# First norm by blocks in turn with small weight pieces, six buffers of weight parts, priorities for some operations, and a merge moved off GpSimd

## The chip, the cores and the metric

The kernel runs on one core of one Trainium2 chip. A core has a matrix engine (TensorE, PE in the profile, with its weight loads as PEld), a vector engine (VectorE, DVE), a scalar engine (ScalarE, ACT), GpSimd (POOL), SyncE (SP, which only issues DMAs here) and 16 DMA engines. Engines run their own instruction queues in order and wait for each other by semaphores. The metric is the device time of one execution in microseconds (us).

## The reference

Two layers (DEPTH 2) of 256 tokens by 1024 channels, float32. Each layer is

```
x = x + 0.5 * swiglu(rmsnorm(x), w_gu (1024 x 5632), w_down (2816 x 1024))
h = rmsnorm(x);  one projection h @ w_in (1024 x 5962)
y_a = 6 heads of attention with forget gates (softmax)
y_b = 5 heads of stick-breaking attention (no softmax; logs and cumulative sums)
y_c = 5 heads of sparse attention (an indexer picks 64 keys a row; softmax)
merged = sig(g_a) * (y_a @ w_up_fox) + sig(g_b) * (y_b @ w_up_sb) + sig(g_c) * (y_c @ w_up_dsa)
x = x + merged @ w_out
x = x + 0.5 * swiglu(rmsnorm(x), ...)        # second pair of weights
```

and a last rmsnorm follows the second layer. All weights, some 205 MB, are read once from HBM as float32.

## The kernel before

**Products.** Every float32 operand of a large product is split into two float16 parts, hi and lo, and the product is three matmuls: hi by hi, hi by lo, lo by hi. `split` (L247) makes the parts: hi on ScalarE (L249), lo on VectorE (L251), for weights (`whi`, `wlo`, read from `raw`) and activations alike. In most products the weight is the stationary operand (a 128 x 128 block) and the activation, 256 tokens wide and transposed (channels on partitions), moves; `project_T` (L317) does these, with three matmuls of 256 columns for each block of weights (L339). `project` (L363) has the tokens stationary.

**Weights.** The list `chunks` (L174) names the weight blocks in the order of use, mostly 1024 rows by 512 columns. Each is cut in raw loads of 4 row blocks (k = 0 to 3, 4 to 7, 1 MB each; the first chunk is cut finer, L206) and each raw load in pieces, at most 2048 columns a partition. `advance(i)` (L274) runs when piece i is about to be used: it emits the splits of the pieces up to i + HL_BUFS, and raw DMAs up to RAW_BUFS ahead of the last split. HL_BUFS is 4 (pairs of parts), RAW_BUFS 5 (L200).

**Order.** The program is laid out by Python; a scheduler then orders each engine's queue, taking among the operations that its own model holds ready the one that was emitted first. `behind` (L143) adds an order edge with no wait. `high_priority`, not used in the kernel before, puts what is emitted in it ahead of earlier emitted work that is ready too. `Task` (L283) wraps a generator of small work; `background()` (L307) steps the first two tasks after every two row blocks of a product (`every`, L349), and `finish` runs one to its end at that place.

**Feed-forward.** `ffn` (L613) computes for each of six column chunks the gate product g, scales it by the row of reciprocal norms R and takes the silu (L632, L633), then the up product u and their product (L638), which is split to `ah`, `al`; then the down product, whose result is added to the transposed residual `xT` (`add_T`, L645 to L649). PSUM tiles: four of tag mm for the products, two tp and two at for the rest.

**Norms.** `Norm.half(h)` (L519) makes `xThi`, `xTlo` of one half of the channels as soon as `xT` is there, without the row scale; `stats` (L529) sums squares, by `acc` (L537, L539) and a matmul (`ss`, L546), takes the power on GpSimd (L469) and `rows_of` (L496) spreads it to R by a matmul (`rb`, L503). `norm.finish()` (L628, L765) forces all of that right after the first product that uses the norm. `FirstNorm` (L581) does the first norm from the untransposed x: `split_half` (L471) transposes four blocks of 128 tokens on PE, applies the gain on VectorE (L483), splits 512 columns, and copies to `xT` (L486); two such for each half of the channels. Five matmuls on an identity (`warm`, L424) precede them.

**Mixer.** `mixer` (L748) runs the groups of w_in, with the attention as tasks: `indexer`, `latent`, `forget` (L916, it ends in the `cps` matmuls, L931), and the heads in pairs. A pair makes its operands `T`, `M`, `W` (`operands`, L795 to L810), yields twice, runs the scores (L833), the softmax (L970, whose last step, L980, scales by the reciprocal sum on VectorE), transposes (L986) and multiplies by the values (L959). Then the gates, the three up products, merged by L1140 and L1142 (the second of three merges on GpSimd), the split to `mT`, and w_out with its residual (L1151).

Of the kernel before, what the change touches and what calls it, by code (L numbers as in the profile page):

```python
# [10 lines left out]
F32 = mybir.dt.float32  # L11
# [118 lines left out]
def trunk(ctx, tc, io, out, flag):  # L130
# [69 lines left out]
    RAW_BUFS, HL_BUFS = (4, 6) if wide else (5, 4)  # L200
    raws, pieces, chunk_pieces = [], [], []
    for ci, (nm, l, r, c, n) in enumerate(chunks):
# [3 lines left out]
        cuts = [0, 1, 2, 4, 6, 8] if ci == 0 else list(range(0, nk, rk)) + [nk]  # L206
# [15 lines left out]
    start, raw_dma = {}, []  # L222
# [33 lines left out]
    def emit_piece():  # L256
# [10 lines left out]
        a, b = split(hv, lv, src, sw, guard and guard.weight())  # L267
        if i in start:
            for j, k in zip((a, b), start[i]):
                behind(j, *k)  # L270
        hl_tiles[i] = (hv, lv)
        state["piece"] += 1

    def advance(i):  # L274

        while state["piece"] < min(len(pieces), i + HL_BUFS):
            emit_piece()
        last = pieces[state["piece"] - 1][0]
        while state["raw"] < min(len(raws), last + RAW_BUFS):
            emit_raw()  # L280
# [141 lines left out]
    warm = att("warm")  # L422
    for i in range(5):
        nc.tensor.matmul(warm[:, :P], ident, ident, start=True, stop=True)  # L424
# [46 lines left out]
    def split_half(src, t, h, hi, lo, gcol, nm, keep):  # L471

        ps = tpt("xp" + nm)
        for j in range(4):
            k = 4 * h + j
            i = nc.tensor.transpose(ps[:, j * P:(j + 1) * P], src[:, t, k * P:(k + 1) * P], ident)
            if h == 1:
                behind(i, state["last"])
        pv = ps.rearrange("p (j c) -> p j c", j=4)
        tmp = t512("xg" + nm)  # L480
        pv2 = tmp.rearrange("p (j c) -> p j c", j=4)
        g = gT[:, gcol + 4 * h:gcol + 4 * h + 4]
        i = nc.vector.tensor_tensor(pv2, pv, g[:, :, None].to_broadcast([P, 4, P]), op=ALU.mult)  # L483
        start.setdefault(0, ((), (i,)))
        r = split(hi[:, 4 * h:4 * h + 4, t * P:(t + 1) * P], lo[:, 4 * h:4 * h + 4, t * P:(t + 1) * P], pv2, 1.0, None)
        behind(nc.scalar.copy(keep, pv), r[0])  # L486
        return r

# [7 lines left out]
    def rows_of(rstd, nm):  # L496

        dg = sp.tile([P, NT, P], F32, tag="kcT", name="dg" + nm)
        for t in range(NT):
            nc.vector.tensor_scalar(dg[:, t, :], ident, rstd[:, t:t + 1], None, op0=ALU.mult)  # L500
        yield
        ps = tpt("rb" + nm)
# [722 lines left out]
```

## Time and profile before

| | |
|---|---|
| median of 3 runs | 1169.36 us (1167.49 to 1169.77) |
| profiled execution | 1170.57 us, of which the span of the trace is 1168.8 |
| busy PE, PEld, DVE, ACT, POOL | 1125.8, 962.6, 792.4, 603.6, 30.0 us |
| mean granted TensorE clock | 0.987 |
| DMA | 209.96 MB, mean 180 GB/s |

Matmuls are pipelined and their ends are modelled: a PE that is busy all of a stretch can still be at half of its rate. How many matmuls a stretch holds, and the clock granted in it, say more. An engine's idle time has a price only where another engine waits for it.

### The profile page before, as it was taken

Reading aid. Unit: us, or ns where it says so; the run is one execution under the profiler, and the core shown is the slowest. Engines: PE = TensorE matmul, PEld = TensorE weight load, DVE = VectorE, ACT = ScalarE, POOL = GpSimd, SP = SyncE. Lnnn points to the kernel's source line nnn. Section 1 sums busy time; section 2 is a strip of 40 time slices with the busy share of each in tenths; the row PEclk is TensorE's granted clock in tenths of the full one; section 3 lists DMA queues with packets and bytes.
Section 4 is the critical chain, followed back from the end, with each engine's and each line's share of the span. In section 5 each row is a group of like instructions: output and inputs, shape, how many; then the busy total and the mean of one; then the engine's idle time right before and its main releaser. Section 6 shows DMA issues by size and latency. Waiting matters only on the chain.

```text
span 1168.8 us, 22864 instructions
## 1 busy us (share of the span) xinstructions
PE 1125.8 (96%) x9736; PEld 962.6 (82%) x9736; DVE 792.4 (68%) x1387; ACT 603.6 (52%) x790; POOL 30.0 (3%) x33
## 2 busy tenths in 40 slices
PE   7999999989999899999999999999999989999996
PEld 5888887777888788888888888867788878888765
DVE  5665655898786866565566565579977698566653
ACT  6544543656566554453454454456556665544531
POOL 0000000000001100000000000000000020000000
PEclk8999999989999999999999999999999999999999
DMA  9755655455434766565656566555453267565731
GB/s 343 239 164 191 227 166 184 147 180 176 132 109 134 230 199 188 161 225 199 217 189 199 163 217 208 163 168 164 166 178 113 91 197 236 182 180 180 245 100 40
DMA packets 118723, 209.96 MB, mean 180 GB/s; under 512 B 4770, under 2 KB 43860, under 8 KB 118612
## 3 DMA queue, kind: packets, MB, share of 16 engines
q1 hardware_dynamic: 118292, 207.88, 55.2%
q8 instruction: 78, 1.28, 0.5%
q10 hardware_dynamic: 320, 0.53, 0.1%
q14 instruction: 33, 0.27, 0.1%
HBM read 207.35 MB, written 1.05 MB: 178 GB/s over the span
## 4 chain that ended last, share of the span: by engine, by line
PE 78%; DVE 13%; ACT 4%; issue 2%; DMA 1%; POOL 0%; POOLq 0%; DVEq 0%; ACTq 0%; SPq 0%
PE uw_ffn_gu L339 20%; PE gw_ffn_gu L339 18%; PE gt L339 9%; PE d0w_ffn_down L339 7%; PE d512w_ffn_down L339 7%; DVE wlo L251 7%; ACT whi L249 3%; PE up L339 2%; PE in L339 2%; PE o L339 1%; PE ya L959 1%; DVE isc L886 1%; DMA raw<-in_w_ffn_gu_dram 1%; PE sa L151 1%; PE in L376 1%
## 5 line engine op out<-in xcount | busy, mean ns | idle before, releaser
L251 DVE SCALAR_TENSOR_TENSOR wlo<-raw,whi 128x2048 f16<-128x2048 f32 (+6 forms) x229 | 459.6, 2009 | 273.0 <-ACT whi L249 267.5
L339 PEld LDWEIGHTS <-whi 128*128 128x128 f16 x5504 | 539.8, 98 | 77.2 <-issue 9.6
L249 ACT ACTIVATE whi<-raw 128x2048 f16<-128x2048 f32 (+6 forms) x229 | 379.1, 1660 | 422.3 <-issue 122.5
L339 PEld LDWEIGHTS <-wlo 128*128 128x128 f16 x2768 | 272.4, 98 | 41.0 <-issue 4.9
L339 PE MATMUL gw_ffn_gu<-xThif,whi 128*128 128x256 f16 x704 | 193.5, 276 | 4.3 <-ACT xThif L249 4.3
L339 PE MATMUL gw_ffn_gu<-xTlof,whi 128*128 128x256 f16 x704 | 194.0, 276 | 1.3 <-DVE xTlof L525 0.7
L339 PE MATMUL uw_ffn_gu<-xThif,whi 128*128 128x256 f16 x704 | 192.0, 273 | 1.9 <-ACT whi L249 1.9
L339 PE MATMUL gw_ffn_gu<-xThif,wlo 128*128 128x256 f16 x704 | 193.7, 276 | 0.0
L339 PE MATMUL uw_ffn_gu<-xThif,wlo 128*128 128x256 f16 x704 | 192.1, 273 | 0.0
L339 PE MATMUL uw_ffn_gu<-xTlof,whi 128*128 128x256 f16 x704 | 192.0, 273 | 0.0
L339 PE MATMUL gt<-xThimx,whi 128*128 128x256 f16 x384 | 104.8, 273 | 0.0
L339 PE MATMUL gt<-xThimx,wlo 128*128 128x256 f16 x384 | 104.7, 273 | 0.0
L339 PE MATMUL gt<-xTlomx,whi 128*128 128x256 f16 x384 | 104.7, 273 | 0.0
L339 PE MATMUL d0w_ffn_down<-ahw_ffn_gu,wlo 128*128 128x256 f16 x264 | 72.0, 273 | 0.0
L339 PE MATMUL d0w_ffn_down<-alw_ffn_gu,whi 128*128 128x256 f16 x264 | 72.0, 273 | 0.0
L339 PE MATMUL d512w_ffn_down<-ahw_ffn_gu,whi 128*128 128x256 f16 x264 | 72.0, 273 | 0.0
L339 PE MATMUL d512w_ffn_down<-ahw_ffn_gu,wlo 128*128 128x256 f16 x264 | 72.0, 273 | 0.0
L339 PE MATMUL d0w_ffn_down<-ahw_ffn_gu,whi 128*128 128x256 f16 x264 | 72.0, 273 | 0.0
L339 PE MATMUL d512w_ffn_down<-alw_ffn_gu,whi 128*128 128x256 f16 x264 | 72.0, 273 | 0.0
L339 PE MATMUL in<-xThimx,whi 128*128 128x256 f16 x176 | 49.2, 280 | 0.0
L339 PE MATMUL in<-xTlomx,whi 128*128 128x256 f16 x176 | 49.0, 278 | 0.0
L339 PE MATMUL in<-xThimx,wlo 128*128 128x256 f16 x176 | 48.9, 278 | 0.0
(328 smaller groups left out, 1376.6 us busy)
## 6 DMA issues: line engine op xcount, KB each, us to landing
raw<-in_w_ffn_gu_dram SPq DMA_DIRECT2D x62, 1024.0 KB, 5.2
raw<-in_w_ffn_down_dram SPq DMA_DIRECT2D x39, 1024.0 KB, 5.1
raw<-in_w_in_dram SPq DMA_DIRECT2D x26, 1024.0 KB, 5.0
raw<-in_w_ffn_gu_dram SPq DMA_DIRECT2D x32, 768.0 KB, 4.6
raw<-in_w_in_dram SPq DMA_DIRECT2D x12, 768.0 KB, 4.4
raw<-in_w_out_dram SPq DMA_DIRECT2D x8, 1024.0 KB, 5.1
raw<-in_w_ffn_down_dram SPq DMA_DIRECT2D x7, 512.0 KB, 3.9
raw<-in_w_in_dram SPq DMA_DIRECT2D x4, 896.0 KB, 4.8
```

Source lines behind the costliest of these rows:

```text
L151: return behind(nc.tensor.matmul(*a, **k), first)
L249: a = nc.scalar.activation(hv, src, AF.Copy, scale=scale)
L251: return a, nc.vector.scalar_tensor_tensor(lv, src, scale, plain(hv), op0=ALU.mult, op1=ALU.subtract, **more)
L339: m = nc.tensor.matmul(o, u, v[:, k, :], start=(k == 0 and q == 0 and b % 2 == 0), stop=(end and q == len(ops) - 1))
L376: state["last"] = nc.tensor.matmul(o, b, wh, start=False, stop=(k == lastk))
L886: nc.vector.match_replace(out=sc[:, a:b], in_to_replace=m8, in_values=sc[:, a:b], imm_value=TAKEN)
L959: m = nc.tensor.matmul(o, v(h, ks), w[:, i * P:(i + 1) * P], start=(i == 0), stop=(i == 2))
```

## The change

- Six buffers of weight parts, HL_BUFS 4 to 6; RAW_BUFS stays 5.
- The first chunk is cut 1, 1, 1, 1, 2, 2 row blocks, the second 2, 2, 2, 2.
- The first norm goes by blocks of 128 channels and all 256 tokens: four transposes for two blocks, hi straight from PSUM on ScalarE with the gain as scale, lo on VectorE, without the separate gain step; each block is followed in both queues by the splits of one weight piece (`begin`). Blocks 4 to 7 begin when row block 3 of the first product is due; until then no more pieces are emitted (`hold`). Copies to `xT` and squares follow after the last block.
- Nine warming matmuls in place of five, and four more after the second set of transposes.
- Of the other norms, parts are emitted with high priority, the sums of squares directly, and the matmuls `ss` and `rb` two background steps later each; a norm is forced only where it is needed (`need`), and the gate's scale and silu of the first chunk are emitted during the u product (`gate`), at the latest at its row block 4.
- High priority for `add_T`, for the merges and splits after the up products, and for the residual after w_out.
- The merge of branch 1 runs on VectorE in place of GpSimd; the softmax's last scaling on ScalarE in place of VectorE.
- Heads yield three times, not two, between operands and scores.

```diff
-    RAW_BUFS, HL_BUFS = (4, 6) if wide else (5, 4)
+    RAW_BUFS, HL_BUFS = (4, 6) if wide else (5, 6)
-        cuts = [0, 1, 2, 4, 6, 8] if ci == 0 else list(range(0, nk, rk)) + [nk]
+        cuts = [0, 1, 2, 3, 4, 6, 8] if ci == 0 else [0, 2, 4, 6, 8] if ci == 1 else list(range(0, nk, rk)) + [nk]
-        while state["piece"] < min(len(pieces), i + HL_BUFS):
+        while state["piece"] < min(state.get("hold", len(pieces)), i + HL_BUFS):
-    for i in range(5):
-        nc.tensor.matmul(warm[:, :P], ident, ident, start=True, stop=True)
+    warm_up(9)
     class Norm:
+        def parts(self, k, src):
+            g = gT[:, self.gcol + k:self.gcol + k + 1]
+            return (nc.scalar.activation(self.hi[:, k, :], src, AF.Copy, scale=g),
+                    nc.vector.scalar_tensor_tensor(self.lo[:, k, :], src, g, plain(self.hi[:, k, :]),
+                                                   op0=ALU.mult, op1=ALU.subtract))
         def half(self, h):
-            for k in range(4 * h, 4 * h + 4):
...
+            with tc.high_priority():
+                for k in range(4 * h, 4 * h + 4):
+                    self.parts(k, xT[:, k, :])
+        def need(self, rows):
+            while self.R is None and (rows or self.rstd is None):
+                self.task.step()
     class FirstNorm(Norm):
+        def block(self, k):
+            q, j = k // 2, k % 2
+            if j == 0:
+                self.ps[q] = (tpt if q < 2 else att)(f"xp{self.nm}_{q}")
+                for i in range(2):
+                    for t in range(NT):
+                        m = nc.tensor.transpose(self.ps[q][:, i * SEQ + t * P:i * SEQ + (t + 1) * P],
+                                                x[:, t, (k + i) * P:(k + i + 1) * P], ident)
+                        if q > 1:
+                            behind(m, state["last"])
+                if q == 1:
+                    warm_up(4, m)
+            r = self.parts(k, self.ps[q][:, j * SEQ:(j + 1) * SEQ])
...
+        def begin(self, ks=range(4)):
+            for k in ks:
+                for r in (self.block(k), state["piece"] < HL_BUFS and emit_piece()):
+                    for i, j in zip(r or (), self.last):
+                        behind(i, j)
+                    self.last = r or self.last
+            if k == 3:
+                state["hold"] = state["piece"]
+            else:
+                self.task = Task(self.stats())
+        def ready(self, k):
+            if k == 3 and state.pop("hold", None):
+                self.begin(range(4, 8))
...
-            norm.finish()
+            def gate(k):
+                if s or (norm.R is None and k < 4):
+                    return
...
-            project_T(gu, l, DFF + c, n, (norm.hi, norm.lo), u)
+            project_T(gu, l, DFF + c, n, (norm.hi, norm.lo), u, gate)
...
-                for i, b, w in widths(n):
-                    add_T(c // P + b, w, d[i], norm.by_row(w))
+                with tc.high_priority():
+                    for i, b, w in widths(n):
+                        add_T(c // P + b, w, d[i], norm.by_row(w))
...
-                nc.vector.tensor_scalar(p[:, a:b], p[:, a:b], rsum[:, i:i + 1], None, op0=ALU.mult)
+                act(p[:, a:b], p[:, a:b], AF.Copy, scale=rsum[:, i:i + 1])
...
-            for _ in range(2):
+            for _ in range(3):
                 yield
...
-                        (nc.gpsimd if b == 1 else nc.vector).tensor_tensor(v0, v0, v, op=ALU.add)
+                            nc.vector.tensor_tensor(v0, v0, v, op=ALU.add)
...
+            with tc.high_priority():
+                for i in range(2):
+                    xs = xT[:, 4 * h + 2 * i:4 * h + 2 * i + 2, :]
+                    nc.vector.scalar_tensor_tensor(xs, pair(ps[i], 2), 1.0 / (sw * sm), xs, op0=ALU.mult, op1=ALU.add)
```

## Rows read from the trace of the kernel before

**Rows 1.** The page's first part: busy us of each engine, share of the span, instructions.
```profile
PE 1125.8 (96%) x9736; PEld 962.6 (82%) x9736; DVE 792.4 (68%) x1387; ACT 603.6 (52%) x790; POOL 30.0 (3%) x33
```

**Rows 2.** Stretches: length, busy us (count) PE, PEld, DVE, ACT, POOL; clock, DMA share, GB/s.
```profile
30.00:135.00 105.00, 105.00 (x961) 93.82 (x960) 68.12 (x94) 52.91 (x49) 0.00 (x0) 1.00 0.64 203
...
280.00:365.00 85.00, 84.33 (x756) 74.07 (x755) 59.95 (x124) 54.04 (x103) 0.00 (x0) 1.00 0.38 121
365.00:405.00 40.00, 35.75 (x324) 31.35 (x322) 35.52 (x51) 21.30 (x22) 8.57 (x4) 1.00 0.72 237
```

**Rows 3.** Chain that ended last, in order of time: start, us, what.
```profile
40.04 10.48 PE gw_ffn_gu L339 x96
```

**Rows 4.** Timeline of the start: start, us, engine, line, operation, count [idle before <-releaser].
```profile
1.82 2.50 PE L424 MATMUL warm<-ident 128*128 128x128 f32 x10 [1.82 <-POOL ident masks.py:199]
...
8.03 0.38 PE L339 MATMUL gw_ffn_gu<-xThif,whi 128*128 128x256 f16 x2 [1.66 <-ACT xThif L249]
...
18.61 0.28 PE L339 MATMUL uw_ffn_gu<-xThif,whi 128*128 128x256 f16 x1 [1.93 <-ACT whi L249]
...
21.83 0.58 PE L339 MATMUL gw_ffn_gu<-xThif,whi 128*128 128x256 f16 x2 [2.61 <-ACT xThif L249]
```

**Rows 5.** One microsecond of the start, columns as in rows 2.
```profile
24.00:25.00 1.00, 1.00 (x7) 0.67 (x6) 0.96 (x4) 0.00 (x0) 0.00 (x0) 0.50 1.05 389
```

**Rows 6.** PE's waits, whole span: line <- releaser: us in total, times, longest.
```profile
PE sa L833 <- DVE Wa L809: 4.1, 2, 2.1
PE o L339 <- DVE wlo L251: 2.9, 2, 1.4
PE o L339 <- DVE mT L251: 2.6, 2, 1.3
PE ssf L546 <- DVE accf L539: 2.5, 3, 1.1
...
PE o L339 <- DVE gt L1140: 1.8, 2, 0.9
PE up L339 <- DVE gt L1140: 1.3, 2, 0.7
...
PE rbmx L503 <- DVE dgmx L500: 1.2, 2, 0.6
PE cps L931 <- issue: 1.1, 1, 1.1
PE cps L931 <- DVE fr L926: 1.1, 1, 1.1
```

**Rows 7.** Four microseconds after three of these waits, columns as in rows 2.
```profile
250.00:254.00 4.00, 4.00 (x17) 3.17 (x16) 3.09 (x9) 1.85 (x5) 0.00 (x0) 0.50 0.66 194
...
418.00:422.00 4.00, 4.00 (x25) 3.16 (x26) 2.21 (x4) 0.00 (x0) 0.70 (x1) 0.65 0.35 133
...
822.00:826.00 4.00, 4.00 (x22) 3.22 (x21) 3.64 (x11) 1.85 (x5) 0.00 (x0) 0.58 0.64 207
```

**Rows 8.** Timeline at the first layer's up products, columns as in rows 4.
```profile
367.13 1.22 DVE L251 SCALAR_TENSOR_TENSOR wlo<-raw,whi 128x1024 f16<-128x1024 f32 x1 [0.51 <-ACT whi L249]
...
370.41 4.02 POOL L1142 TENSOR_TENSOR gt<-gt 128x512 f32<-128x512 f32 x2 [147.42 <-DVE gt L1140]
...
373.23 2.29 DVE L251 SCALAR_TENSOR_TENSOR wlo<-raw,whi 128x1024 f16<-128x1024 f32 x1
```

**Rows 9.** Groups of instructions, shapes apart: count | busy us, mean ns | idle before.
```profile
L251 DVE SCALAR_TENSOR_TENSOR wlo<-raw,whi 128x512 f16<-128x512 f32 x10 | 6.8, 683 | 6.2 <-PE cb L151 4.9 <-ACT whi L249 1.3
...
L525 DVE SCALAR_TENSOR_TENSOR xTlof<-xT,gT,xThif 128x256 f16<-128x256 f32 x24 | 10.0, 479 | 0.0
...
L980 DVE TENSOR_SCALAR pa<-pa,rsa 128x256 f32<-128x256 f32 x12 | 4.2, 346 | 0.0
...
L759 ACT ACTIVATE pa<-sa,nxa 128x256 f32<-128x256 f32 x12 | 5.6, 467 | 3.5 <-DVE nxa L975 3.5
```

**Rows 10.** ACT's longest waits within the softmax, columns as in rows 6.
```profile
ACT pc L759 <- DVE nxc L975: 11.3, 14, 1.7
```

## What the change was predicted to do, before its result was known

> **What bounds the kernel now.** I read the busy totals first. PE is busy 96% of the span and no other engine reaches 70% [rows 1]; so what counts is where PE does not run at its rate. The rate is in the chain that ended last: 96 matmuls in 10.48 us, 0.109 us each [rows 3]. The table by stages then says where this holds. From 30 to 135 us PE is busy all the time at clock 1.00, with VectorE at 68 of 105 us [rows 2]: here nothing can be gained but by doing less work. In the attention with the gates (280 to 365) PE misses 0.7 of 85 us. Around the up products (365 to 405) PE misses 4.3 of 40 us while VectorE is busy 35.5: that stretch is VectorE's [rows 2]. The start and the joints between stages are the third kind, so I read the timeline of the start and then the list of PE's waits.
>
> A busy PE can hide lost time. The Trainium skill ("Perfetto Trace Analysis", section Identifying the Most-Contended Engine) says to judge TensorE's headroom by the busy share of its weight loads, not of its matmuls. The steady stretch has 93.82 of 105 us, 0.894, the whole 962.6 of 1168.8, 0.824 [rows 1, 2]: by that rule some 92 us are off the steady rate, where PE's idle time gives 43. Part of it is matmuls of another shape, so I take neither as what can be won; I count waits one by one.
>
> The profiled execution took 1170.57 us (span 1168.8 and 1.8 around it), 1.2 above the median of 1169.36. The sum is made against 1170.57.
>
> **A. The start.** The second gate chunk begins at 40.04 [rows 3]. Before it lie two chunks of 96, 21.0 us of matmuls, and the first of them begins at 8.03 [rows 4]; so 11.0 us are lost in between. Two holes are plain: a wait of 1.93 for a weight part that ScalarE makes 2048 columns at a time, and one of 2.61 for the second half of the norm, which had been queued behind it [rows 4]. PE then runs at clock 0.50, that is 1.2 of 2.4 GHz, for example 7 matmuls between 24 and 25 us [rows 5]. DMA is no bound: 389 GB/s there [rows 5], and x and two chunks are 5 MB, 13 us.
> After the change each block of 128 channels costs VectorE one lo of 256 columns, 0.48, and one weight part of 512, 0.68 [rows 9], 1.16 in all, and ScalarE about as much; PE needs 12 x 0.109 = 1.31 for it. So PE is the slowest of the three, narrowly, and once started should not wait. The start itself does not come earlier. Five warming matmuls are ten records in 2.43 us (1.82 to 4.25) [rows 4]; nine hold PE until 1.82 + 4.4 = 6.2. Four transposes at that pace end at 7.2, hi takes 0.47 (ScalarE, 256 columns) and the first weight part about 0.68 [rows 9]: 8.3. Added to that: 21.0 of matmuls, 1.5 for transposes, the second warming and the R matmul (estimated at the warming's pace or twice it), 0.5 for the first lo parts. The second gate chunk then starts at 31.3: **-8.7**. Bounds: a start at 7.8 with no ramp, 30.3, -9.7; five more us at half clock (2.5) and one wait as long as the old one (2.6), 36.4, -3.6.
>
> **B. The first scores of the mixer.** In both layers PE waits for VectorE's operands of the first pair of heads, 4.1 us in two waits, and behind it for `cps`, 1.1 + 1.1 [rows 6]; 6.3. PE's clock then falls to 0.50 and 0.58 for four us [rows 7]: 2.0 + 1.7 lost. Ten us in all. The extra yield puts two row blocks of products ahead of the scores, about 2 x 9 x 0.109 = 2.0 us, as long as one of the waits; two more buffers let VectorE have two more weight parts done by then, 2.4 us of its time at 1.22 for each 1024 columns [rows 8]. The forget gate's chain to `cps` is not shortened, so I leave a part: **-7.0**; bounds 0 (the wait is only moved) and -10.0.
>
> **C. The up products and w_out.** PE waits there 2.9 for weight parts, 2.6 for `mT`, 1.8 and 1.3 for the merge's first step: 8.6 in two layers [rows 6]. All are VectorE's. What it gains: two parts ahead. What the GpSimd merge cost it: a split of 1024 columns took 2.29 beside the merge, 1.22 without [rows 8], 1.07 more; four splits of each layer lie beside the merges, so at most 4.3 a layer. What it gets: four merges of 512 columns a layer, 0.68 each by the nearest row of that width [rows 9], 2.7. So the move is about even to 1.6 better, and it takes 2.0 us for each add (4.02 for two [rows 8]) down to 0.7 in the chain. The priority is worth more: merge and `mT` no longer wait behind splits of weights that PE needs only later. But VectorE stays nearly full, so some of it comes back as a wait for weights: **-6.0**; bounds 0 and -8.6.
> The Trainium skill ("SBUF — State Buffer", section Who interferes with whom) says more than the row: an operation of VectorE with two inputs in SBUF and one of GpSimd that reads SBUF shut each other out for a whole instruction. The row's split gained 1.07, not the whole of an add of 2.0; it began in mid-merge, so it decides little. By the rule C would be at its end, -8.6, and the sum 1143.5.
>
> **D. Norms at the joints.** PE waits for the sums of squares, 2.5 in three waits, and for the rows of R, 1.2 in two [rows 6]; after the first mixer its clock falls to 0.65 for four us [rows 7], 1.4 lost. 5.1 in all. Priority brings the parts forward by up to one split of weights; `ss` and `rb` come four row blocks later in PE's queue, 4 x 1.31 = 5.2 us, more than any of the waits. Late next is the gate's multiplication, behind row block 2 or 4 of u; the next gate product that needs its banks starts four to six row blocks later, over 5 us, so that is covered. **-3.8**; bounds -0.5 and -5.1.
>
> **E. What is new and unseen.** The softmax's scaling leaves VectorE, 0.346 for 256 columns, and costs ScalarE about the 0.467 of an exponential of that width [rows 9], 44 operations. In the stage it has 31 us of 85 free [rows 2], so it costs nothing while that cover holds. Six buffers ask for splits earlier, which may stand before attention operands that got no priority. Copies to `xT` and squares follow the first norm beside splits. I take **+1.0**; bounds -2.0 (VectorE freed within the attention) and +6.0 (one wait of 1.5 in each of four joints).
>
> Sum: -8.7 - 7.0 - 6.0 - 3.8 + 1.0 = -24.5; 1170.57 - 24.5 = 1146.1, and 1144.9 beside the median. I predict 1145.0. All good ends: -35.4, 1135.2; all bad ends: +1.9, 1172.5.
>
> **Rivals.** (1) The queues come out as before within the mixer: priority only orders what the scheduler's model holds ready at once, and a split already running is not stopped. Then B and C fall to nothing: 1146.1 + 13.0 = 1159.1. For it: VectorE is full there anyhow [rows 2]. Against: three of the four waits in C are for operations that the text emitted late, not for work that is missing. Chance 0.14.
> (2) The start does not shrink: thirteen warming matmuls, twenty-six records at 0.24, stand on PE ahead of the first product, and a block's turn waits for its weight load. Only 3.6 of A is won: 1151.2. For it: VectorE's 1.16 against 1.31 leaves little. Chance 0.10.
> (3) Slower: ScalarE's scaling stands in its queue waiting for VectorE's reciprocal, which stands behind a weight split, and the weight's hi parts stand behind it. ScalarE has 54.0 busy in 85 [rows 2] and gets 22 x 0.47 = 10.3 a layer; with a wait w for each of 11 heads it becomes the bound from w = 20.7/11 = 1.9 us. At 3.5, one and a half splits, it is 54.0 + 10.3 + 38.5 - 85 = 17.8 late a layer, 35.6 in both: 1181.7. Against: the same handing over exists now, and ScalarE's waits for the row maxima are 11.3 in 14, 0.8 each, the longest 1.7 [rows 10]. Chance 0.05.
> (4) It does not do what it says, all bad ends together: waits move, none goes, 1172. Chance 0.04.
>
> **How the numbers follow.** The forecast, 1145, has 0.67, and its own range is 1136 to 1156. About 0.2% is what a measurement of this kernel can tell from no change, 2.3 us. Forecast and rivals 1 and 2 are faster: 0.91. Rival 4 lies within 0.2% or close by: same 0.04. Rival 3 is slower: 0.05. The range takes in the good ends nearly whole and rival 1 on the other side: 1135 to 1160.
>
> **What would show it.** A: the second gate chunk starts at 30 to 33 us, with no PE wait over 1 us between its first matmul and that. B: the wait of `sa` for `Wa` under 1 us a layer, and a clock near 1.00 in the four us behind it. C: no add on GpSimd, PE's waits in w_out under 1.5 us a layer, and weight splits of 1024 columns at 1.22. D: `ss` and `rb` without a wait. E: ScalarE's waits for the reciprocal at or below 0.8 each. The prediction is wrong if the steady chunks (96 in 10.48) change, if new PE waits in the attention exceed 5 us, or if the start saves less than 4.

## The result and the profile after

The change takes 1161.41 us (median of 20 runs, 1158.57 to 1168.45), the kernel before 1169.14 beside it: ratio 0.9941, 95% interval 0.9929 to 0.9954. So it is faster, by 7.7 us; I had predicted 1145.0 and a range from 1135 to 1160.

The profiled execution of after took 1166.04 us (span 1164.2), 4.6 above the median, and that of before 1170.57, 1.4 above its own. The two traces therefore account for 4.5 of the 7.7 us. The single runs of after differ by the clock granted to PE: 1158.57 us at a mean of 0.995, 1168.45 at 0.984, the profiled one at 0.987, so its trace shows more time at the lower level than most of the twenty.

The page's first part, after (compare [rows 1]):

```profile
PE 1126.7 (97%) x9752; PEld 964.2 (83%) x9752; DVE 776.9 (67%) x1357; ACT 618.8 (53%) x841; POOL 12.9 (1%) x25
```

PE's waits over the whole span, after: us in total, times, longest (compare [rows 6]):

```profile
PE ssf L520 <- DVE accf L509: 4.1, 3, 1.9
PE cps L946 <- issue: 3.7, 1, 3.7
PE cps L946 <- DVE fr L941: 3.6, 1, 3.6
PE rbf L546 <- DVE dgf L542: 2.9, 1, 2.9
...
PE ppa L1001 <- ACT pa L774: 1.7, 4, 0.5
...
PE o L337 <- DVE mT L251: 1.0, 2, 0.6
PE up L337 <- DVE gt L1157: 1.0, 2, 0.5
```

PE's waits in the up products and w_out fell from 8.6 to 2.0, and those of `sa` are gone. In their place stand 7.3 for `cps` (2.2 before), 4.1 for the sums of squares (2.5) and 2.9 for the first norm's R (0.9 before). For `issue` the profile shows no releaser; `cps` starts 0.1 behind `fr` there as in the other layer.

Where the time went shows in the stages. The first fence is the windows by stage of before, the second those of after: `in` to the gates, up products and w_out (first layer), then the second feed-forward from its first gate product to its second gate chunk, in either layer. Columns as in [rows 2].

```profile
192.12:274.13 82.01, 76.89 (x564) 57.24 (x561) 73.63 (x202) 49.80 (x97) 3.52 (x3) 0.96 0.53 167
...
362.45:410.15 47.70, 43.45 (x395) 38.26 (x393) 41.56 (x60) 27.95 (x32) 8.57 (x4) 1.00 0.65 209
410.15:435.41 25.26, 24.13 (x204) 20.75 (x202) 16.83 (x26) 12.94 (x14) 0.70 (x1) 0.93 0.57 189
...
981.13:1005.73 24.60, 23.47 (x213) 20.77 (x211) 17.63 (x30) 13.83 (x16) 0.70 (x1) 1.00 0.61 196
```

```profile
189.38:268.79 79.41, 72.93 (x553) 54.83 (x551) 72.16 (x189) 49.79 (x95) 3.52 (x3) 0.98 0.56 178
...
357.79:403.89 46.10, 44.98 (x404) 39.30 (x402) 42.44 (x68) 34.66 (x42) 0.00 (x0) 1.00 0.60 202
403.89:431.72 27.83, 25.90 (x205) 21.92 (x203) 19.28 (x28) 13.08 (x14) 0.69 (x1) 0.88 0.67 234
...
973.60:1002.55 28.95, 26.81 (x212) 22.79 (x210) 20.30 (x32) 13.96 (x16) 0.69 (x1) 0.88 0.67 225
```

The third number is the length of the stage. The joints after the mixer grew by 2.57 and 4.35, at a clock of 0.88; the mixers, from `in` to the end of w_out, shrank by 3.52 and 2.74 (some ten matmul records moved from the first of these stages into the last). The start shrank by 2.7, the first feed-forward's joint in layer 2 by 1.1, the end by 1.4, and the steady stretches not at all (152.25 against 152.24). The sum is -4.6, the difference of the spans.

How much a joint costs depends on whether the clock falls in it. e12 below changes only the softmax, and its first joint has the same wait for the sums of squares; the clock stays at 1.00 and the joint is 3.3 shorter than in after, 0.7 shorter even than before. The timeline and the window of that joint in e12:

```profile
412.13 1.05 PE L520 MATMUL ssf<-ones,accf 128*128 128x2 f32 x8 [1.93 <-DVE accf L509]
```

```profile
402.22:426.74 24.52, 22.59 (x204) 19.87 (x203) 19.27 (x28) 13.16 (x15) 0.69 (x1) 1.00 0.77 268
```

### The profile page after: what moved, and what is told of

Same layout as the page of the kernel before. It is cut to its first block, busy times and chain, and to the rows that moved or that the text cites. A ratio compares the mean times of both kernels' runs of the same rounds, so it can differ in the third digit from the quotient of the medians.

```text
span 1164.2 us, 22885 instructions
## 1 busy us (share of the span) xinstructions
PE 1126.7 (97%) x9752; PEld 964.2 (83%) x9752; DVE 776.9 (67%) x1357; ACT 618.8 (53%) x841; POOL 12.9 (1%) x25
## 3 DMA queue, kind: packets, MB, share of 16 engines
q8 instruction: 78, 1.28, 0.4%
## 4 chain that ended last, share of the span: by engine, by line
PE 76%; DVE 13%; ACT 5%; issue 3%; DMA 1%; POOL 1%; POOLq 0%; DVEq 0%; ACTq 0%
PE uw_ffn_gu L337 19%; PE gw_ffn_gu L337 17%; PE d0w_ffn_down L337 7%; PE gt L337 7%; PE d512w_ffn_down L337 7%; DVE wlo L251 7%; PE in L337 3%; ACT whi L249 3%; PE up L337 1%; DMA raw<-in_w_ffn_gu_dram 1%; PE in L374 1%; PE in L372 1%; PE in L373 1%; DVE xTlof L493 1%; PE ya L974 1%
## 5 line engine op out<-in xcount | busy, mean ns | idle before, releaser
L251 DVE SCALAR_TENSOR_TENSOR wlo<-raw,whi 128x2048 f16<-128x2048 f32 (+7 forms) x232 | 452.7, 1954 | 268.4 <-ACT whi L249 267.7
L249 ACT ACTIVATE whi<-raw 128x2048 f16<-128x2048 f32 (+7 forms) x232 | 379.2, 1640 | 400.6 <-issue 136.6
```

What stands on the lines that cost most here:

```text
L249: a = nc.scalar.activation(hv, src, AF.Copy, scale=scale)
L251: return a, nc.vector.scalar_tensor_tensor(lv, src, scale, plain(hv), op0=ALU.mult, op1=ALU.subtract, **more)
```

## The experiments

All medians are of runs beside the kernel before (1168.6 to 1169.7). Ratios are to it.

| kernel | us | ratio (95%) |
|---|---|---|
| the change | 1161.4 | 0.9941 (0.9929 to 0.9954) |
| e1 four buffers | 1162.5 | 0.9957 (0.9941 to 0.9973) |
| e2 no priority | 1166.2 | 0.9977 (0.9966 to 0.9987) |
| e3 before, with six buffers | 1172.2 | 1.0024 (1.0014 to 1.0033) |
| e4 start | 1157.6 | 0.9897 (0.9880 to 0.9913) |
| e5 forget gate's matmul later | 1173.0 | 1.0044 (1.0027 to 1.0060) |
| e6 joint | 1151.8 | 0.9865 (0.9848 to 0.9881) |
| e7 e4, e5 and e6 | 1166.0 | 0.9978 (0.9969 to 0.9988) |
| e9 e7 with five buffers | 1168.0 | 0.9997 (0.9987 to 1.0007) |
| e10 e4 and e6 | 1149.1 | 0.9829 (0.9813 to 0.9846) |
| e11 e6, gate with priority | 1152.9 | 0.9856 (0.9840 to 0.9873) |
| e14 e10, gate with priority | 1149.5 | 0.9833 (0.9817 to 0.9849) |
| e16 e10, gate's end on GpSimd | 1152.5 | 0.9860 (0.9836 to 0.9883) |
| e17 e10, gate and scores later | 1167.7 | 0.9988 (0.9978 to 0.9998) |
| e18 e10, one chunk in half splits | 1149.7 | 0.9835 (0.9817 to 0.9853) |
| e19 e10, all splits halved | **1142.3** | 0.9771 (0.9754 to 0.9789) |
| e12 softmax scaling back on VectorE | 1160.3 | 0.9923 (0.9898 to 0.9948) |
| e13 merge back on GpSimd | 1158.3 | 0.9908 (0.9892 to 0.9925) |
| e15 two yields | 1157.8 | 0.9902 (0.9878 to 0.9926) |

### What each part of the change is worth

```diff
e1, from the change
-    RAW_BUFS, HL_BUFS = (4, 6) if wide else (5, 6)
+    RAW_BUFS, HL_BUFS = (4, 6) if wide else (5, 4)
e2, from the change, in four places
-            with tc.high_priority():
+            with ExitStack():
e3, from the kernel before
-    RAW_BUFS, HL_BUFS = (4, 6) if wide else (5, 4)
+    RAW_BUFS, HL_BUFS = (4, 6) if wide else (5, 6)
```

> The changed kernel with four buffers of weight parts, all else as changed. Theory 1 (crowding): with six buffers VectorE always has a ready split of 2.3 us to begin, and awaited operations start behind it; with four, PE's wait of ssf falls from 4.1 to under 2.5 us in all, the wait of cps from 3.7 to about 1 a layer, and the time is at or under 1161. Theory 2 (place): the waits come from where the change puts ss, rb and cps in PE's queue; then they stay, w_out's waits for weight parts come back (up to 2.9), and the time is 1163 to 1167.

> The changed kernel without its four priority blocks. If priority is what took the 8.6 us of waits at the up products and w_out down to 2.0, they come back and the time is 1165 to 1169. If the two more buffers or the merge on VectorE did it, the waits stay near 2 us and the time is within 1159 to 1163.

> The kernel before with six buffers of weight parts and nothing else. Theory 1 (crowding): no gain, 1167 to 1174, with awaited operations of VectorE later and waits of PE for Wa, mT and acc at least as long. Rival (the buffers are the gain): w_out's 2.9 us wait for weight parts goes and the time is about 1164.

With four buffers the median is 1.1 us higher, which the two intervals do not tell apart. PE waits 8.6 for weight parts in the up products (5.1 for `wlo`, 3.5 for `whi`), but only 0.2 for the sums of squares and not at all for the first R, and the second gate chunk begins at 32.40 (first matmul), where the change has 37.13. So six buffers trade a shortage for crowding, nearly one for one. `cps` still waits 3.6 and 3.4: my first theory held for the sums and not for `cps`. In the kernel before, two more buffers alone make it slower by 3: `sa` waits no more, but `cps` 7.4 and w_out 5.8 for the merge. Without priority PE's waits in the up products and w_out are 8.8 again, and the time rises by 4.8. So priority is what carries term C.

```diff
e12, from the change
-                act(p[:, a:b], p[:, a:b], AF.Copy, scale=rsum[:, i:i + 1])
+                nc.vector.tensor_scalar(p[:, a:b], p[:, a:b], rsum[:, i:i + 1], None, op0=ALU.mult)
e13, from the change
-                            nc.vector.tensor_tensor(v0, v0, v, op=ALU.add)
+                            (nc.gpsimd if b == 1 else nc.vector).tensor_tensor(v0, v0, v, op=ALU.add)
e15, from the change, in three places
-            for _ in range(3):
+            for _ in range(2):
```

> The change with the softmax's last scaling back on VectorE. By term E the move is free on ScalarE and frees VectorE 44 times 0.35 = 15 us, where VectorE bounds only part of the time: 1161 to 1165, the waits for p in the transposes (1.7 and 1.0) going or moving to VectorE. Rival: the move costs more than it gives, since ScalarE's scale stands behind weight parts of 1.9 us: 1157 to 1160. Second rival: VectorE's relief is what the gains in the up products rest on: over 1166, with waits there over 5 us.

> The change with one line undone: the merge of branch 1 back on GpSimd, still under high priority. By my sum the move itself was about even to 1.6 us better a layer in VectorE's time, and the add itself 2.0 against 0.7 in the chain, so of the 6.6 us of waits that went from the up products and w_out only 1 to 3 belong to the move: 1162 to 1165, GpSimd's adds of 2.0 us back, weight splits beside them at 1.8 to 2.3 in place of 1.22. Rival: the whole of the 6.6 is the move, by the two engines no longer shutting each other out: 1167 to 1169, with waits of the up products and w_out of 7 or more again. Second rival: GpSimd relieves the fuller VectorE more than it hinders it: 1158 to 1161.

> The change with the heads' yields put back from three to two. By term B the extra yield carries a good part of the 4.1 us that PE waited for the first scores' operands before: sa waits again for 2 to 4 us in two layers, 1164 to 1167. Rival: the two more buffers and the later cps did it alone (in the kernel before with six buffers the wait for the scores' operands was gone too): no wait for the operands over 0.5, 1159 to 1163.

The softmax's place makes no difference that these runs can tell. Undoing the merge or the yield makes the kernel about 3 us *faster*, against both of my first expectations; the intervals part by only 0.0003 to 0.0004 of the ratio. For e13 the time is in the range of my second rival, but GpSimd's relief of VectorE does not show: the two mixers are longer (216.3 each against 214.5 and 214.4), and the joints behind them shorter (23.18 and 23.78 against 27.83 and 28.95). PE's waits in these two kernels, e13 first:

```profile
PE o L337 <- DVE mT L251: 3.9, 2, 2.0
...
PE ssf L520 <- DVE accf L509: 0.2, 1, 0.2
```

```profile
PE o L337 <- DVE mT L251: 3.2, 2, 1.6
...
PE ssf L520 <- DVE accf L509: 0.2, 1, 0.2
```

Undoing either costs 2 to 3 us of waits at `mT`, and loses all but 0.2 of the 4.1 for the sums of squares, which neither touches. That wait hangs on where the splits happen to lie when the joint comes. With two yields `sa` does not wait for `Wa` either, nor with three yields and four buffers (e1): the yield was not needed to remove that wait.

### The start and the joints

e4 gives ScalarE a tiny copy at the very start, so that its table is loaded while it idles, and emits the four squares right behind block 3.

```diff
e4, from the change
+    nc.scalar.activation(negur[:, :2], ident[:, :2], AF.Copy)
...
+                self.ss = sp.tile([P, NT, 2], F32, tag="ss", name="ss" + self.nm)
+                for h in range(2):
+                    for t in range(NT):
+                        behind(square(...), self.last[0])
...
-                for t in range(NT):
-                    behind(square(...), copy)
-            yield
```

> The changed kernel with a tiny ScalarE copy at the very start, so that the table load is not behind the gains, and with the first norm's four squares emitted right after block 3, so that the reciprocal norms are ready early. Theory: the start lost 1.3 us to the table load and 2.9 us plus half clock to the R matmul's wait; then the first product starts at about 7.6, the R matmul has no wait, the second gate chunk starts at 32 to 33 in place of 37.3, and the time falls by about 5 to 1156. Rival: what is won at the start is lost again at the next shortage (raw loads of 1 MB, landing late), and the time stays above 1159.

The second gate chunk begins at 33.00 in place of 37.30, the wait for R is gone, and the median falls by 3.9, about as the theory had it. The order of the squares is what counts. The early table load lets the first `xThif` begin at 7.32 in place of 7.83, when the transposes release it, but the first product begins at 8.82 in place of 8.88, right behind the second warming in either kernel. And 37.30 holds 1.6 of clock lost behind the wait, which need not come: e6 below has the start of the change too, with a wait of 2.4 for R and clock 1.00 behind it. Its second gate chunk:

```profile
35.69 10.64 PE gw_ffn_gu L337 x96
```

```diff
e6, from the change, in the sums of squares of a norm
+            with tc.high_priority():
                 for i in range(2):
                     sq = t512(f"sq{self.nm}_{h}{i}")
                     nc.scalar.activation(...)
...
+            yield
```

> The changed kernel with the squares and sums of the norms given priority too, and ss one background step later. Theory: the 1.9 us waits of ssf in both layers go, and with them the half clock after (3 us in the first layer's profile); 1155 to 1158, and runs spread less than 1158.6 to 1168.5. Rival: a weight split that is already running or that the scheduler's model sees ready first stands in front all the same; ssf stays over 1 us and the time within 1160 to 1163.

9.6 us less, more than the theory's range and the largest gain of one edit. The timeline of the first of these joints, VectorE and then PE, in the change:

```profile
406.03 2.28 DVE L251 SCALAR_TENSOR_TENSOR wlo<-raw,whi 128x2048 f16<-128x2048 f32 x1
...
410.42 0.68 DVE L509 TENSOR_TENSOR accf<-accf,sqf 128x512 f32<-128x512 f32 x1
411.02 2.28 DVE L251 SCALAR_TENSOR_TENSOR wlo<-raw,whi 128x2048 f16<-128x2048 f32 x1
...
413.23 0.68 DVE L509 TENSOR_TENSOR accf<-accf,sqf 128x512 f32<-128x512 f32 x1
...
413.97 1.80 PE L520 MATMUL ssf<-ones,accf 128*128 128x2 f32 x8 [1.93 <-DVE accf L509]
```

and in e6:

```profile
406.98 0.68 DVE L510 TENSOR_TENSOR accf<-accf,sqf 128x512 f32<-128x512 f32 x1
...
407.98 0.69 DVE L510 TENSOR_TENSOR accf<-accf,sqf 128x512 f32<-128x512 f32 x1
...
409.37 2.29 DVE L251 SCALAR_TENSOR_TENSOR wlo<-raw,whi 128x2048 f16<-128x2048 f32 x1
```

In the change two splits of weights stand in the chain to the sum; in e6 only the one between the residuals does, the next split follows the sums, and PE does not wait for it in that joint. The edit has two halves, which no run separates: the sum is ready 7.0 us into the joint in place of 10.0, and `ss` is due at 10.6 in place of 8.1. By these times either half alone would have removed the wait there. Behind the wait the clock falls. Windows of the change, then the whole joint in e6:

```profile
416.00:420.00 4.00, 4.00 (x20) 2.87 (x19) 0.91 (x7) 0.00 (x0) 0.69 (x1) 0.50 1.04 393
984.00:988.00 4.00, 4.00 (x20) 3.29 (x21) 3.21 (x10) 0.00 (x0) 0.69 (x1) 0.51 0.89 278
```

```profile
402.00:418.00 16.00, 16.00 (x149) 14.32 (x147) 14.88 (x23) 8.26 (x9) 0.69 (x1) 1.00 0.91 323
```

Summed over windows of 4 us, (1 - clock) x 4, the change loses 6.8 us of clock in these two joints, the kernel before 1.7, e6 nothing. So the wait of 1.93 in the first joint cost 5.5 us where the clock fell (27.83 in the change, 22.32 in e10 below, which has no wait) and 2.2 where it did not (24.52 in e12).

> The joint edit and the start edit together, the forget gate left as the change has it. If the two holes are independent, their gains add: the joint gained about 9.6 against the change (1151.8 against 1161.4), the start 3.9 (1157.6), so 1148 +-1.5, with the second gate chunk beginning at 33.0 us, no wait for the R matmul of the first norm and none over 0.5 us for the sums of squares; the two waits for cps stay at 3.6 to 3.7 each. Rival: part of the joint's gain was luck of the queues in that one program (every edit reorders them), and the sum comes out at 1151 to 1155, with waits of over 1.5 us at places that neither edit touches.

The two edits together give 1149.1 where their gains added make 1148: as far as these medians tell, the holes are independent.

### The forget gate: the wait that moves

PE stands for 3.6 to 3.7 before `cps` in each layer. In the timeline of the change, VectorE, with the window around it:

```profile
241.89 0.17 DVE L933 TENSOR_TENSOR f<-pr,bfor 128x12 f32<-128x12 f32 x1
...
242.81 2.28 DVE L251 SCALAR_TENSOR_TENSOR wlo<-raw,whi 128x2048 f16<-128x2048 f32 x1
...
245.02 0.17 DVE L939 SCALAR_TENSOR_TENSOR f<-f,fe 128x12 f32<-128x12 f32 x1
...
245.65 0.27 DVE L941 COPY fr<-f 128x36 f32<-128x36 f32 x2
```

```profile
240.00:256.00 16.00, 12.30 (x96) 10.12 (x94) 15.63 (x43) 8.87 (x15) 0.00 (x0) 0.89 0.70 233
```

A split lies in the chain, and VectorE is busy 15.63 of 16 us. My theory was the split; the rivals were the place of `cps` and VectorE's fullness.

```diff
e5, from the change
             yield
+            yield
+            yield
             cps = tpt("cps" + L)
...
-            t_f.finish()
             if 0 not in yT:
...
             for _ in range(3):
                 yield
+            t_f.finish()
             kb, qb = X["kb"], X["qb"]
e17, from e10: as e5, and behind the moved finish
+            yield
+            yield
e11, from e6, and e14, from e10: both halves of forget()
+            with tc.high_priority():
e16, from e10
-            nc.vector.scalar_tensor_tensor(f, f, 0.0, e, op0=ALU.min, op1=ALU.subtract)
+            nc.gpsimd.tensor_scalar(f, f, 0.0, None, op0=ALU.min)
+            nc.gpsimd.tensor_tensor(f, f, e, op=ALU.subtract)
...
-                nc.vector.tensor_copy(fr[:, :, o:o + 18]...)
+                nc.gpsimd.tensor_copy(fr[:, :, o:o + 18]...)
e18, from e10
-        pk = rk // 2 if wide else rk
+        pk = rk // 2 if wide or c == GATES else rk
```

> The changed kernel with the cps matmuls two background steps later and forced only ahead of the scores, which puts some 54 matmuls (5.9 us) before them in PE's queue. Theory 2 (place): the forget gate's chain (VectorE, ScalarE, VectorE) is the bound there, whatever the number of buffers or yields; given 5.9 us, the waits of cps, 3.7 in each layer, fall under 0.5, the half clock behind them goes (about 1.6 a layer), and the time is 1161.4 - 7 to 10, 1151 to 1155. Theory 1 (VectorE is simply full there): the wait moves to the scores or to the next weights, and the time is above 1158.

> The edits of the start, of the forget gate and of the norms together, six buffers. If PE's waits are separate losses, the gains add: 4 + 7 + 4 under 1161.4, so 1146 to 1149. If PE only waits elsewhere for the same work of VectorE, it is over 1152.

> The same three edits with five buffers. Crowding by six against shortage by four (8.6 us of waits for weights at the up products with four): if both matter, five lies within 2 us of six; if shortage rules, five is 3 to 5 us slower.

> The joint and start edits together; cps two background steps later and the first scores of every pair of the forget heads two steps later as well, so that the chain from cps to the scores keeps its distance. Theory: only the place of cps in PE's queue is wrong; with two steps (4 to 5 us) more of products ahead of it the waits of 3.7 go and nothing takes their place, with the clock behind them at 1.00: 1149.1 less 7 to 11, 1138 to 1142. Rival: VectorE has no room left in this stretch, so the waits come back at the scores (qb), the values or the merges, as where cps alone was put later (7.2 for qb, 3.8 for mT): 1149 to 1160.

Later is worse each time, by 8.7 to 8.9 us for each mixer in e5 (223.2 against 214.5 and 214.4). Five buffers come out 2.0 slower than six (e9, e7). PE's waits in e17:

```profile
PE sa L151 <- DVE qb L967: 7.8, 2, 3.9
PE o L337 <- ACT mT L249: 4.0, 2, 2.0
...
PE cps L951 <- issue: 0.8, 1, 0.8
```

The 3.7 leaves `cps` and comes back at the scores, and more comes at w_out. With five buffers (e9) `cps` waits 3.8 and 3.7 even so.

> The joint edit, and both halves of the forget gate's chain under high priority, nothing moved. Theory: what cps waits for is a weight split of 2.28 us that VectorE places between the two steps of the gate while ScalarE does its exponentials; with priority that split waits, the two waits fall from 3.7 to 1.4 or less each, the clock behind them stays near 1.00, and the time is 1145 to 1148 against the joint edit's 1151.8. Rival 1: the priority decides nothing, since the split is the only operation ready while ScalarE works and VectorE takes it anyway: waits 3.6 to 3.7, 1151 to 1153. Rival 2: the wait goes to the next operands, as where cps was put two steps later: cps under 1.5, but the scores wait 2 to 3.6 a layer for their operands, 1150 to 1156.

> The joint edit, the start edit and the forget gate's priority together. If the three holes are independent and the priority works: 1148 (joint and start) less 4 to 6 for two waits of 3.7 that fall to 1.4 with the clock behind them, 1141 to 1145, which would also be about the time that I predicted for the change. Rival: the priority decides nothing, 1147 to 1149.5. Rival 2: what is taken from one place comes back at another, 1150 to 1156, with new waits of over 2 us in the mixer.

Rival 1 came out: priority decides nothing (waits 3.6 to 3.7). In e11 it brings the gate's first step forward by 1.2 us, but the split still goes ahead of the second, and `fr` is ready 55.80 us after the mixer's first matmul, as in e10.

> The joint and start edits together, and the last steps of the forget gate (minimum, subtraction, the two copies to fr) on GpSimd, which is idle, in place of VectorE. Theory: the weight split of 2.28 us in VectorE's queue is what the chain waits for; four small operations of GpSimd at 0.3 to 0.7 each take its place, so the waits for cps fall from 3.7 to 2 to 3 each and the time from 1149.1 to 1146 to 1148.5. Rival: cps stands too early in PE's queue whatever VectorE does, because a weight part of 1.9 us on ScalarE stands in the chain as well and GpSimd's operations are slow: 3.5 or more each, 1148.5 to 1151.

The rival's side, and beyond its range: the waits grew to 5.2 each. VectorE and GpSimd in e16:

```profile
237.79 2.27 DVE L251 SCALAR_TENSOR_TENSOR wlo<-raw,whi 128x2048 f16<-128x2048 f32 x1
...
237.96 2.17 POOL L943 TENSOR_TENSOR f<-f,fe 128x12 f32<-128x12 f32 x1 [0.31 <-ACT fe L777]
```

A subtraction of 12 columns takes 2.17, in the second layer too, and ends with the split that began 0.17 before it. The split stays in the chain although it is on another engine. But that is not why the wait grew: in the first layer `fr` is ready 55.49 us after the mixer's first matmul, against 55.80 in e10, and PE comes to `cps` after 356 matmuls in place of 373, 17 times 0.109 or 1.9 us earlier. So the edit moved `cps` in PE's queue as well, and of the place and the chain it tests only the chain: GpSimd took 0.3 off it.

> The joint and start edits together; the first chunk of the gates is split in pieces of 1024 columns in place of 2048 (4 pieces for 2), nothing else. Theory: the gate's chain to cps holds one split of ScalarE (1.91) and one of VectorE (2.28) that cannot be interrupted; halved they take about 1.06 and 1.22, so each wait for cps falls from 3.6 by 1.1 to 1.9, to 1.7 to 2.6, and the time from 1149.1 to 1145 to 1147.5. Rival: two halves run one after the other in the same gap and the chain is as late as before: waits 3.4 or more, 1148.5 to 1150.

The rival came out. No split lies between the gate's two steps here, but one half stands before the first. The chain ends 0.4 earlier than in e10 (55.39), and three matmuls fewer (370) stand ahead of `cps`, which takes 0.3 back. VectorE, then PE:

```profile
237.09 1.21 DVE L251 SCALAR_TENSOR_TENSOR wlo<-raw,whi 128x1024 f16<-128x1024 f32 x1
...
238.50 0.16 DVE L936 TENSOR_TENSOR f<-pr,bfor 128x12 f32<-128x12 f32 x1
...
240.81 2.05 PE L949 MATMUL cps<-c_tri,fr 128*128 128x256 f32 x4 [3.60 <-issue]
```

So my theory fell: the split between the steps is not the cause by itself. What the change, e18 and e19 have in common is that 5.0 to 5.5 us pass from the end of `pr`, on ScalarE, to the end of `fr`, and that VectorE is busy in all but 0.1 of them. Which of that work could wait (the sorting for the indexer, splits, operands of later heads) was not tried and stays open.

### Shorter splits everywhere

```diff
e19, from e10
-    RAW, PIECE = 2048, 1024 if wide else 2048
-    RAW_BUFS, HL_BUFS = (4, 6) if wide else (5, 6)
+    RAW, PIECE = 2048, 1024
+    RAW_BUFS, HL_BUFS = (4, 6) if wide else (5, 12)
...
-        pk = rk // 2 if wide else rk
+        pk = max(2, rk // 2)
...
-                for r in (self.block(k), state["piece"] < HL_BUFS and emit_piece()):
+                for r in (self.block(k), state["piece"] < 6 and emit_piece()):
```

> The joint and start edits together; all weights split in pieces of at most 1024 columns, with twelve buffers of half the size, so the bytes held ahead are the same. Theory: a split in the way costs its own length, so halved splits halve the waits that are left (cps 3.7 to 2, kin 1.2 to 0.7, mT and gt), against 2 x 1.22 - 2.28 = 0.16 us more of VectorE for each of some 200 splits, 32 us where VectorE has 370 idle: 1143 to 1148. Rival: the added time falls where VectorE is full (attention's end, up products, w_out), and more splits become ready at once and run ahead of the other operations: 1152 to 1160 with waits of over 3 us in the up products and w_out.

1142.3, below the theory's range and 6.9 under e10. PE's waits in e10 and then in e19:

```profile
PE cps L949 <- issue: 3.7, 1, 3.7
PE cps L949 <- DVE fr L944: 3.6, 1, 3.6
...
PE ppa L1004 <- ACT pa L777: 1.7, 4, 0.5
...
PE o L337 <- DVE mT L251: 1.0, 2, 0.6
PE up L337 <- DVE gt L1160: 1.0, 2, 0.5
```

```profile
PE cps L949 <- issue: 3.2, 1, 3.2
PE cps L949 <- DVE fr L944: 3.2, 1, 3.2
```

The waits for `mT` and `gt` and that of `ppa` for the softmax's `pa` are gone from the list, the one for `kin` falls from 2.4 to 1.7, and two of 1.2 are new or longer (`ppc` for `Tc`, `sa` for `qb`). All waits but the first warming's sum to 20.0 in e10 and 14.1 in e19, 5.9 of the 6.3 between the two spans (1147.4 and 1141.1). VectorE pays for it, 798.4 us busy against 776.0 in e10, where PE does not feel it. As I read it, a wait for an operation behind a split costs up to the split's length, and e19 shortens that length in all places at once; `cps` moves by only 0.4 to 0.5. A rival is not tested: with half the length a buffer also comes free, and a product gets its first part, after half the time. e19 is 1.65% faster than the change (1142.27/1161.41) and the fastest of all these kernels.

## Why the prediction was wrong

The direction held, and so did C. A and B were too large, and D gained nothing. Of the 19.9 between the forecast's -24.5 and the -4.6 of the two traces, A has 6.0, B, C and E together 5.7, and D 9.6, less 1.4 that the end gained and that I had not counted. The steps that failed are named below, each with what the runs showed in its place.

**A, -8.7 forecast, -2.7 found.** The chain of after:

```profile
37.30 10.48 PE gw_ffn_gu L337 x96
```

against 40.04 [rows 3] and 31.3 forecast, outside my bound of 36.4; where the clock stays at 1.00 behind the wait, as in e6, it is 35.69, and some 4.3 is found. The step that failed is "once started should not wait". The timeline, ScalarE, VectorE, PE:

```profile
6.54 1.28 ACT L492 ACT_TABLE_LOAD   x1 [6.54 <-DVE gT L416]
7.83 0.47 ACT L492 ACTIVATE xThif<-xpf,gT 128x256 f16<-128x256 f32 x1
...
27.22 2.29 DVE L251 SCALAR_TENSOR_TENSOR wlo<-raw,whi 128x2048 f16<-128x2048 f32 x1 [3.72 <-ACT whi L249]
...
29.44 0.15 DVE L617 TENSOR_TENSOR gms<-ssf 128x2 f32<-128x2 f32 x1
...
31.46 0.88 PE L546 MATMUL rbf<-dgf,ones 128*128 128x256 f32 x2 [2.93 <-DVE dgf L542]
```

The blocks kept their turn. But I priced the R matmul as a matmul and not as the end of a chain: the squares stand behind a split on ScalarE, the statistics behind its `wlo`, PE waits 2.93, and from 32 to 36 us its clock is 0.60, 1.6 more. It is the two more buffers that bring that split forward: with four (e1) the squares are done at 23.95 in place of 28.42, and R is not waited for. e4 shows the same by the order alone: 33.00. The start itself was mis-sized by 0.6: the first product begins at 8.88, not 8.3. ScalarE's first instruction now needs `gT`, so its table load of 1.28, which ran at 1.19 us in idle time before, stands behind that wait and ahead of the first `xThif`; but with the load out of the way (e4) the first product begins only 0.06 earlier. The Trainium skill ("ScalarE: Activation LUTs", section What ACT_TABLE_LOAD costs) gives 1283 ns for the load, as here, and 1380 ns of drain with it for a switch to a different set; this trace shows no drain: its seven later loads begin 0.02 behind one activation, and all eight end 0.01 before the next.

**B, -7.0 forecast, little of it found.** The step that failed is "the forget gate's chain to `cps` is not shortened, so I leave a part". The two waits for `sa` went, the first check I had named, but the waits of the stage as a whole rose from 6.3 to 7.3, and the second check failed (clock 0.72 from 248 to 252 us). The fault was to look for a wait by its name and not at their sum: what I left for that chain was not a part but all of it. What came from the stage is clock, 5.1 lost before and 3.4 after. The extra yield was not needed for `sa` (e15), and in e3 six buffers had the same wait for `cps` without it. The bound "0, the wait is only moved" was the right one, as rival 1 had it for B.

**C, -6.0 forecast; waits -6.6 found.** From 8.6 to 2.0. The weight splits of 1024 columns take 1.218 on average in place of 1.341, the merges 0.68. Priority is worth most of it (e2: 8.8 of waits without), the merge's move 2.9 at `mT` (e13). With the merge back on GpSimd, still with priority, the splits of 1024 stay at 1.217: there the two engines' clash costs them nothing. What it cost in the kernel before, where they took 1.341, no run separates.

The mixers as a whole gained 6.3 where B, C and E made 12.0: PE's idle time in them fell by 2.0 (other waits, those for `cps` and in the softmax above all, eat most of C's), the clock gave 1.7, and 2.5 lie in stretches where PE is recorded as busy, which I can't split up.

**D, -3.8 forecast; +5.8 found in this trace** (+2.57, +4.35, and -1.10 in the first feed-forward of layer 2). The step that failed is "`ss` and `rb` come four row blocks later in PE's queue, 4 x 1.31 = 5.2 us, more than any of the waits". In both joints after a mixer `ss` stands behind 72 matmuls of the joint in place of 59 and is due 1.5 to 1.8 later, while the sum that it waits for is ready 2.3 to 2.6 later (10.0 us into the first joint, before 7.7). "Priority brings the parts forward by up to one split" holds for the parts, but the squares' sums got none and fell behind them: without priority (e2) the sum is ready at 8.9. And the two more buffers, which I counted only as a gain for B and C, make splits ready that fill VectorE to 12.00 of 12 us from 404 to 416. With four buffers (e1) the sums are waited for 0.2 in all. I had this as "+6.0, one wait of 1.5 in each of four joints" among the bounds of E and gave it +1.0. It was two waits of 1.9, and 5.1 more of lost clock, which I had not priced. The lost clock is most of the +5.8, and in e12's first joint the same wait brought none; without it D is about +0.7, an estimate from 5.8 and 5.1, and still no gain. The rows of R are waited for as before, 1.2 in two.

**E apart from that:** PE has small waits of 2.7 for `pa` and `pc`, but with the scaling back on VectorE (e12) 2.2 stand for `pa`, and the time shows no difference. My mark of 0.8 for each of ScalarE's waits for the reciprocal was missed: 9.5 in 8, the longest 2.0, and 1.5 in 4. **The rivals:** 3's long waits did not come; these 11.0 are 0.5 for each of 22 heads, where it needed 1.9. 1 had B right and C wrong. 2 came near the size of A, 3.6, but not to its cause: with the same warming matmuls e4 starts the second gate chunk at 33.00.

With the joints and the start mended, e10, the time is 1149.1: A and D were there to be had, 12.3 us of them, and hung on a few lines that the change lacked. B was not, in any of these runs.

## What to carry to other kernels

Where one engine makes the operands of all stages, price each split by its length in the way of every operation that is awaited. Halving that length gave 6.9 us here; deeper buffers alone cost 3 (e3), and in the change they brought waits for the sums and for R that one small edit each took away. Judge a removed wait by the sum of the waits in its stage, and give a wait of about 2 us on PE two prices, with the clock that it may lose behind it and without (5.5 and 2.2 here). When an edit moves one operation, count what now stands ahead of the awaited one in the other queue too: in e16 the chain got shorter and the wait longer.

## What the hardware showed that I had not expected

- A GpSimd subtraction of 12 columns took 2.17 us beside a split of VectorE with two inputs, 2.27. The Trainium skill ("SBUF — State Buffer", section Who interferes with whom) has it so that an operation of VectorE with two inputs in SBUF and one of GpSimd that reads SBUF contend, and that the first to issue decides who blocks; this trace agrees, the split not being slowed. Moving a small step to an idle GpSimd was no way round a busy VectorE here.
- A wait of 1.93 on PE was followed in the change by 4 us at clock 0.50, the lower of the two levels, and in e12, before the same matmuls, by clock 1.00. In e6, where PE works through, the same stretch has 1.00.
